# One input tile for all sublayers, U4 ahead of the first transposes, and the memory's products ahead of their stage, in a twelve-sublayer transformer kernel

## The chip, the cores and the metric

The kernel runs on one core of a Trainium2 chip. The metric is the device time of one execution in microseconds (us). A profile is one more execution, taken with the hardware profiler.

## The reference

Three blocks of four sublayers work on one sequence x of 256 rows by 1024 columns, all in float32. Every sublayer normalises x, computes, and adds its result to x:

- block 1: feed-forward f00, convolution module, f01, f10, the gated recurrence hgrn2, f11
- block 2, with shift, scale and gate made from a conditioning vector (adaln): g00, dsa (indexer-selected attention), g01, g10, diff (differential attention), g11
- block 3: pool with attention to a memory of 256 rows, feed-forward m0, moba with attention to the memory, feed-forward m1

What matters here:

```
def swiglu_ffn(x, w_in, w_out):          # f.. and g..: width 2816 or 2752
    gate, up = jnp.split(x @ w_in, 2, axis=-1)
    return (jax.nn.silu(gate) * up) @ w_out

def mem_cross_attention(qm, mem_n, w_mem_kv, q_gain, k_gain):   # in pool and moba
    k, v = jnp.split(mem_n @ w_mem_kv, 2, axis=-1)
    q = rms_norm_3(qm.reshape(B, S, MEM_HEADS, HEAD_DIM), q_gain)
    k = rms_norm_3(k.reshape(B, M, MEM_HEADS, HEAD_DIM), k_gain)
    ...
    p = jax.nn.softmax(s, axis=-1)
    return jnp.einsum('bhsm,bmhd->bshd', p, v)
```

mem_n is the memory normalised with the sublayer's own gain, so the memory's keys and values do not depend on x.

## The kernel before, in words

**Chunks.** All weights are packed into 413 chunks of 1 MB, in the order in which the program takes them (`_plan`, `_ffn_plan`). A U chunk is 1024 rows by 256 columns of an input weight, a W chunk is half of the rows of 512 such columns (two W make two U blocks), and a V chunk is 256 rows by 1024 columns of an output weight. SP's queue loads a chunk into one of three raw buffers (L292). To multiply at close to float32 precision, `_split` makes two parts of each: ACT copies it, rounded, to hi in four pieces of 512 columns (L305), VectorE subtracts, lo = raw - hi, in eight pieces of 256 (L308). There are five buffers of hi and lo each. Every matrix product is three: hi with the input's high part, lo with the high part, hi with the input's low part.

**Products.** The stage's input is the pair `act`, xh and xl: x normalised, transposed to columns and split. A U product (`proj_u`, L517 to L519) has the weight as the stationary operand and gives 128 hidden columns of gate and up for all 256 rows; a chunk has 48 of them. The first four hidden blocks of a stage are made the other way round (`first` and `proj_pair`, L547 to L549): the input is stationary, in two passes, rows 0 to 127 (m = 0) and rows 128 to 255 (m = 1), 48 products each. The second half of the input is needed only in the second pass, and is transposed while the first runs (`split_t(1, ...)`, issued ten products before the pass ends). Their results have rows on partitions, so these four blocks are transposed after Silu and multiplication (L716 to L718), split (L663, L664) and so become the stationary operand hh, hl of the V products (`down`, L588). V products add up in four PSUM banks, and the last four chunks are held back: `finish` runs them for rows 0 to 127, then for rows 128 to 255, and while the second half runs, x of the first is updated, normalised (L413, L418, L419, L460) and, behind the tenth product from the end, transposed (L475) and copied into the next stage's input (L483 and L484, or eight smaller copies L488 and L489 where a shift is added).

**Input tiles.** `new_act` allocates a new pair xh, xl in a pool with one place for each. It is called at the start, for each next stage in `finish`, and in four mixers besides for the output that goes into the output product. A new tile in a place waits until everything that used the old one is done.

**Order in a feed-forward stage.** `ffn` runs `first` (blocks 0 to 3), transposes and splits the hidden blocks 0 to 3, then V0, U4, U5, V1, U6, U7, V2 and so on. In the first and second block's stages it also lets VectorE make adaln's vectors (L1076), piece by piece between chunks.

**The memory.** Its rows are normalised and transposed in the stage before (`mem_norm`, in `first`). `mem_kv` multiplies them (48 products L547 to L549 into ps), copies keys and values out (L1510, L1511), normalises the keys per head (L1462, L394 to L402, L1468, L1474) and transposes them (`to_heads`, L1169, L1174); then it closes the memory's pool, whose place the pool of the stage's own tiles takes over. In `pool` it stands before `first`, in `moba` behind it. moba then makes its keys and queries: copy out (L1191), rotation (L1158 to L1162), norms, transposes, then the next pair's products, chunk pair 2 first.

**Order of the work.** A scheduler orders each engine's instructions ahead of time, from program order and an estimate of when each is ready. An engine then takes its list strictly in order. `issue_after` and `issue(products, n, then)` hold what `then` issues behind the n-th product. `high_priority(300)` lifts the memory's query in `pool` ahead of some other work.

Of the kernel before, what the change touches and what calls it, by code (L numbers as in the profile page):

```python
# [64 lines left out]
def _plan(stages):  # L65
    p = []
    for s in stages:
# [200 lines left out]
class _K:  # L268
# [27 lines left out]
    def _split(self):  # L296
# [9 lines left out]
        for p in range(self.LP):  # L306
            c = slice(2048 // self.LP * p, 2048 // self.LP * (p + 1))
# [32 lines left out]
    def consts(self, act):  # L340
# [29 lines left out]
        self.pending = self.normed(self.x[:, 1], pre)  # L370
# [137 lines left out]
    def proj_u(self, w, act, nb=2):  # L508

        wh, wl = w  # L510
        xh, xl = act
        p = self.ps()
        for b in range(nb):
            o = p[:, 256 * b:256 * b + 256]
            for k in range(8):
                c = slice(256 * k + 128 * b, 256 * k + 128 * b + 128)
                self.nc.tensor.matmul(o, lhsT=wh[:, c], rhs=xh[:, k, :], start=(k == 0), stop=False)  # L517
                self.nc.tensor.matmul(o, lhsT=wh[:, c], rhs=xl[:, k, :], start=False, stop=False)  # L518
                self.nc.tensor.matmul(o, lhsT=wl[:, c], rhs=xh[:, k, :], start=False, stop=(k == 7))  # L519
        return p  # L520
# [106 lines left out]
    def first(self, s, pairs, act):  # L627
# [4 lines left out]
        for m in range(2):  # L632
# [6 lines left out]
            if m == 0:  # L639
# [28 lines left out]
    def ffn(self, s, act):  # L668
        nc, tc = self.nc, self.tc
        nf = 22  # L670
        with tc.tile_pool(name="hp_" + s, bufs=2) as hp:
# [37 lines left out]
            for g in range(2):  # L709
                p = self.ps("tr")  # L710
                for b in range(2):
                    sg = hp.tile([128, 2, 128], F32, name="sg")
                    h = hp.tile([128, 2, 128], F32, name="h")
                    for m in range(2):
                        pp = p4[2 * g + b][m]
                        nc.scalar.activation(sg[:, m], pp[:, :128], AF.Silu)  # L716
                        nc.vector.tensor_tensor(h[:, m], sg[:, m], pp[:, 128:], op=OP.mult)
                        nc.tensor.transpose(p[:, 256 * b + 128 * m:256 * b + 128 * m + 128], h[:, m], self.ident)  # L718
                groups[g] = self.split(p, hp)
            acc = self.new_acc()  # L720
            self.rows_ahead(s)
            for g in range(1, 11):
                for f in (2 * g, 2 * g + 1) if g > 1 else ():
                    w = self.take(("U", s, f))
                    more()
                    hidden(f, self.proj_u(w, act, 1 if s[0] == "g" and f == nf - 1 else 2))
                if g < 8:
                    w = self.take(("V", s, g - 1))
                    more()
                    for m in range(2):  # L730
                        self.down(m, acc[m], w, hs(g - 1), (128, 128), g == 1, False)
# [769 lines left out]
    def mem_kv(self):  # L1501
# [12 lines left out]
        self.scaled(k, rs)  # L1514
        self.to_heads(k, kT)
        self.mem_inner.close()
        return kT, v
# [68 lines left out]
    def moba(self, act):  # L1586
        nc, tc = self.nc, self.tc
        p4 = self.first("moba", _U_ORDER["moba"][:2], act)
        self.rows_ahead("moba")
        kTm, vm = self.mem_kv()  # L1590
        with tc.tile_pool(name="mb", bufs=2) as mp:
# [10 lines left out]
            def key(pp):  # L1602
# [4 lines left out]
                t = mp.tile([128, 2, S], F32, name="kT")  # L1607
                self.to_heads(x, t)
                return t

            def query(pp):
# [3 lines left out]
                t = mp.tile([128, 2, S], F32, name="qT")  # L1615
                self.to_heads(x, t)
                return t, qs
# [105 lines left out]
```

## Time and profile before

| | us |
|---|---|
| median of 3 runs | 2679.16 |
| lowest, highest | 2674.89, 2680.54 |
| the profiled execution | 2686.03 |
| its span, from first to last instruction | 2684.3 |
| VectorE's lo subtractions (L308), 3304 of them | 1188.1 |
| ACT's hi copies (L305), 1652 of them | 945.8 |
| U products (L517 to L519), 8352 of them | 789.7 + 789.0 + 788.3 |
| V products of feed-forward blocks (L588), 2880 of them | 314.6 + 312.9 + 311.1 |

In the profile PE is TensorE, PEld its weight loads, DVE is VectorE, POOL is GpSimd, SP issues the DMAs. A line of a timeline gives start and duration in us, engine, source line, operation, output<-inputs with their shapes, how many instructions are merged into the line, and in brackets how long the engine had been idle before and what it waited for. Neighbouring products overlap in the profile, so their pace is read from their starts. A line of the waits gives engine, operation and line, what was waited for, the total in us, how often, and the longest. A line of the stretches gives the stretch, its length, the busy time and count of PE, PEld, DVE, ACT and POOL, then the granted TensorE clock as a share of full speed, the DMA engines' busy share and GB/s. The averages hide that stages have different limits: what a change is worth is read at the place.

### The profile page before, as it was taken

How to read it: one execution, taken by the hardware profiler on the slowest of the kernel's cores; microseconds unless marked ns; L12 is line 12 of the kernel's file. 1: busy time of each engine (PE TensorE's matmuls, PEld its weight loads, DVE VectorE, ACT ScalarE, POOL GpSimd, SP SyncE). 2: the span in 40 equal slices, each digit the busy share in tenths (PEclk: the TensorE clock that was granted, in tenths of full speed). 3: DMA queues.
4: the chain of work that ended last, by engine and by line, in shares of the span. 5: the costliest groups of instructions: out<-in, count | busy, mean ns of one | idle time of the engine just before them, and what ended most of it. 6: DMA issues, size and time to landing. Idle time of an engine off the chain costs nothing.

```text
span 2684.3 us, 43506 instructions
## 1 busy us (share of the span) xinstructions
PE 2628.1 (98%) x15984; PEld 2307.8 (86%) x15984; DVE 1960.1 (73%) x5536; ACT 1377.8 (51%) x3054; POOL 103.7 (4%) x200
## 2 busy tenths in 40 slices
PE   8999999999999999999999999999999999999999
PEld 7998789989988899899779989977799789877898
DVE  7858887587588885886879678677855866577764
ACT  5445354454554544644665454455644554455543
POOL 0004200000000000000000000000000000000000
PEclk9999899999999999999999999999999999999999
DMA  8744166476434675784448668653554455442452
GB/s 327 291 157 143 65 253 254 173 275 252 156 145 158 252 282 189 266 307 173 173 159 316 240 233 325 219 191 126 206 187 173 169 182 194 173 167 95 175 186 94
DMA packets 91159, 543.62 MB, mean 203 GB/s; under 512 B 10541, under 2 KB 11581, under 8 KB 38082
## 3 DMA queue, kind: packets, MB, share of 16 engines
q1 hardware_dynamic: 90946, 540.85, 55.4%
q8 instruction: 125, 2.05, 0.3%
q14 instruction: 88, 0.72, 0.1%
HBM read 539.69 MB, written 1.13 MB: 201 GB/s over the span
## 4 chain that ended last, share of the span: by engine, by line
issue 46%; PE 42%; DVE 7%; ACT 2%; DMA 2%; POOL 1%; SPq 0%; POOLq 0%; DVEq 0%; ACTq 0%
PE a L588 16%; PE ps L517 7%; PE ps L519 7%; PE ps L518 7%; DVE lo L308 3%; DVE y L828 2%; PE a L548 1%; PE a L549 1%; PE a L547 1%; DMA raw<-in_wall 1%; POOL ry L419 1%; ACT hi L305 1%; ACT junk L413 1%; DMA xn<-modd 1%; DVE xn L460 1%
## 5 line engine op out<-in xcount | busy, mean ns | idle before, releaser
L308 DVE TENSOR_TENSOR lo<-raw,hi 128x256 fp32r<-128x256 f32 x3304 | 1188.1, 419 | 402.4 <-ACT hi L305 402.0
L305 ACT ACTIVATE hi<-raw 128x512 fp32r<-128x512 f32 x1652 | 945.8, 623 | 810.1 <-PE ps L518 269.1
L517 PE MATMUL ps<-xh,hi 128*128 128x256 f32 x2784 | 789.7, 284 | 0.0
L518 PE MATMUL ps<-xl,hi 128*128 128x256 f32 x2784 | 789.0, 283 | 0.0
L519 PE MATMUL ps<-xh,lo 128*128 128x256 f32 x2784 | 788.3, 283 | 0.0
L518 PEld LDWEIGHTS ps<-xl,hi 128*128 128x128 f32 x2784 | 533.3, 192 | 3.8
L517 PEld LDWEIGHTS ps<-xh,hi 128*128 128x128 f32 x2784 | 533.5, 192 | 3.4
L519 PEld LDWEIGHTS ps<-xh,lo 128*128 128x128 f32 x2784 | 533.7, 192 | 0.5
L588 PE MATMUL a<-hi,hh 128*128 128x512 f32 x960 | 314.6, 398 | 2.4 <-ACT hh L663 2.4
L588 PE MATMUL a<-lo,hh 128*128 128x512 f32 x960 | 312.9, 397 | 0.0
L588 PE MATMUL a<-hi,hl 128*128 128x512 f32 x960 | 311.1, 396 | 0.0
L588 PEld LDWEIGHTS a<-lo,hh 128*128 128x128 f32 x960 | 180.3, 188 | 43.5 <-issue 0.2
L588 PEld LDWEIGHTS a<-hi,hl 128*128 128x128 f32 x960 | 180.2, 188 | 43.4
L547 PE MATMUL a<-hi,xh 128*128 128x512 f32 x512 | 203.4, 397 | 8.1 <-ACT xh L483 5.7
L588 PEld LDWEIGHTS a<-hi,hh 128*128 128x128 f32 x960 | 175.0, 188 | 39.5 <-ACT hh L663 3.4
L549 PE MATMUL a<-hi,xl 128*128 128x512 f32 x512 | 202.7, 399 | 1.7 <-DVE xl L489 1.0
L1076 DVE SCALAR_TENSOR_TENSOR adaj<-adaw,cond 128x1024 bf16<-128x1024 f32 x144 | 175.8, 1221 | 37.9 <-DMA adaw<-in_ada 36.7
L548 PE MATMUL a<-lo,xh 128*128 128x512 f32 x512 | 201.6, 394 | 0.5 <-DVE lo L308 0.5
L547 PEld LDWEIGHTS a<-hi,xh 128*128 128x128 f32 x512 | 97.2, 190 | 33.4 <-ACT xh L483 7.4
L549 PEld LDWEIGHTS a<-hi,xl 128*128 128x128 f32 x512 | 96.9, 189 | 27.5 <-DVE xl L484 4.2
L548 PEld LDWEIGHTS a<-lo,xh 128*128 128x128 f32 x512 | 97.1, 190 | 21.8 <-DVE lo L308 1.8
L438 DVE TENSOR_TENSOR upd<-a,pg 128x512 f32<-128x512 f32 x48 | 33.0, 688 | 73.6 <-ACT junk L413 73.6
(352 smaller groups left out, 2743.0 us busy)
## 6 DMA issues: line engine op xcount, KB each, us to landing
raw<-in_wall SPq DMA_DIRECT2D x413, 1024.0 KB, 4.8
adaw<-in_ada SPq DMA_DIRECT2D x144, 512.0 KB, 6.3
G<-in_rows SPq DMA_DIRECT2D x16, 512.0 KB, 4.5
pg<-in_rows SPq DMA_DIRECT2D x12, 512.0 KB, 4.5
xn<-modd SPq DMA_DIRECT2D x12, 512.0 KB, 4.4
cond<-condd SPq DMA_DIRECT2D x7, 512.0 KB, 5.9
memt<-in_mem SPq DMA_DIRECT2D x4, 512.0 KB
x<-in_x SPq DMA_DIRECT2D x2, 512.0 KB, 8.3
```

The source lines that it names most:

```text
L305: self.nc.scalar.activation(h[:, c], r[:, c], AF.Copy)
L308: self.nc.vector.tensor_tensor(l[:, c], r[:, c], h[:, c].bitcast(F32), op=OP.subtract)
L438: nc.vector.tensor_tensor(t, acc[n], pg[:, s], op=OP.mult)
L517: self.nc.tensor.matmul(o, lhsT=wh[:, c], rhs=xh[:, k, :], start=(k == 0), stop=False)
L518: self.nc.tensor.matmul(o, lhsT=wh[:, c], rhs=xl[:, k, :], start=False, stop=False)
L519: self.nc.tensor.matmul(o, lhsT=wl[:, c], rhs=xh[:, k, :], start=False, stop=(k == 7))
L547: yield self.nc.tensor.matmul(p, lhsT=xh[:, k, t], rhs=wh[:, c], start=(k == 0), stop=False)
L548: yield self.nc.tensor.matmul(p, lhsT=xh[:, k, t], rhs=wl[:, c], start=False, stop=False)
L549: yield self.nc.tensor.matmul(p, lhsT=xl[:, k, t], rhs=wh[:, c], start=False, stop=(k == 7))
L588: mm = lambda l, r, i, st, sp: nc.tensor.matmul(acc[i], lhsT=l[:k, t], rhs=r[:k, 1024 * b + 512 * i:1024 * b + 512 * i + 512], start=st, s ...
L828: nc.vector.scalar_tensor_tensor(c, hp[:, j, t:t + S], w(t), c, op0=OP.mult, op1=OP.add)
L1076: self.nc.vector.scalar_tensor_tensor(junk, self.ada_w.pop(n), 1.0, self.cond, op0=OP.mult, op1=OP.mult, accum_out=self.mods[k][:, c:c + 1])
```

## The change

Five edits. (1) `new_act` makes the pair once and returns the same objects ever after. (2) In the feed-forward stages of f and g kind, U4 comes directly behind the first four blocks; their transposes and splits are issued behind U4's 20th product, then V0, U5, V1 and on as before. Silu and multiplication of all four blocks stand ahead of that; their results lie in two places of the hh and hl buffers. (3) In `pool` and `moba` the memory's products and norms come first, then the stage's `first`, then the transposes of the memory's keys; moba multiplies chunk pair 2 before it transposes its first keys and queries. (4) In the six mixers, memory chunks included, lo is made in four pieces of 512 columns. (5) At the start both halves of x are transposed before the first product in program order, and `first` of f00 issues none.

```
@@ _ffn_plan: W(0,1) W(2,3) U4 V0 U5 V1 U6 U7 V2 ...
+        if g == 2:
+            out.insert(-1, ("V", tag, 0))
-        if 0 < g < ng - 3:
+        if 1 < g < ng - 3:
             out.append(("V", tag, g - 1))
@@ _plan
-                at = 4 if s == "moba" else 0
-                us[at:at] = _w("mem0" if s == "pool" else "mem1", 0, 1)
+                us[:0] = _w("mem0" if s == "pool" else "mem1", 0, 1)
@@ _split
-        for p in range(self.LP):
-            c = slice(2048 // self.LP * p, 2048 // self.LP * (p + 1))
+        lp = self.LP if self.plan[i][1][0] in "fg" or self.plan[i][1] in ("m0", "m1") else self.LP // 2
+        for p in range(lp):
+            c = slice(2048 // lp * p, 2048 // lp * (p + 1))
             self.nc.vector.tensor_tensor(l[:, c], r[:, c], h[:, c].bitcast(F32), op=OP.subtract)
@@ consts
-        self.pending = self.normed(self.x[:, 1], pre)
+        self.split_t(1, self.normed(self.x[:, 1], pre), act)
+        self.pending = None
@@ new_act
-        return (self.act.tile([128, 8, 256], F32R, name="xh"), self.act.tile([128, 8, 256], F32R, name="xl"))
+        if self.the_act is None:
+            self.the_act = (self.act.tile([128, 8, 256], F32R, name="xh"), self.act.tile([128, 8, 256], F32R, name="xl"))
+        return self.the_act
@@ proj_u: its loop is now the generator u_products
+        p = self.ps()
+        self.issue(self.u_products(w, act, p, nb))
+        return p
@@ first
-            if m == 0:
+            if m == 0 and self.pending:
@@ ffn
-            for g in range(2):
-                p = self.ps("tr")
-                for b in range(2):
...
-                        nc.tensor.transpose(p[:, 256 * b + 128 * m:256 * b + 128 * m + 128], h[:, m], self.ident)
-                groups[g] = self.split(p, hp)
-            acc = self.new_acc()
+            hts = []
+            for f in range(4):
+                sg = hp.tile([128, 2, 128], F32, name="sg")
+                if f % 2 == 0:
+                    ht = hp.tile([128, 2, 2, 128], F32, name="hh" if f == 0 else "hl", bufs=4)
+                h = ht[:, f % 2]
+                for m in range(2):
+                    pp = p4[f][m]
+                    nc.scalar.activation(sg[:, m], pp[:, :128], AF.Silu)
+                    nc.vector.tensor_tensor(h[:, m], sg[:, m], pp[:, 128:], op=OP.mult)
+                hts.append(h)
+            def turn():
+                for g in range(2):
+                    p = self.ps("tr")
+                    for b in range(2):
+                        for m in range(2):
+                            nc.tensor.transpose(p[:, 256 * b + 128 * m:256 * b + 128 * m + 128], hts[2 * g + b][:, m], self.ident)
+                    groups[g] = self.split(p, hp)
...
+                    products = self.u_products(w, act, p, 1 if s[0] == "g" and f == nf - 1 else 2)
+                    if f == 4:
+                        self.issue(products, 20, turn)
+                    else:
+                        self.issue(products)
+                    hidden(f, p)
+                    if f == 4:
+                        acc = self.new_acc()
+                    if f == 4 or (f % 2 and g < 8):
+                        j = 0 if f == 4 else g - 1
+                        w = self.take(("V", s, j))
...
@@ mem_kv ends ahead of the transposes
+        return k, kT, v
+
+    def mem_keys(self, k, kT):
         self.to_heads(k, kT)
         self.mem_inner.close()
@@ pool
-        kT, v = self.mem_kv()
+        k, kT, v = self.mem_kv()
+        p4 = self.first("pool", _U_ORDER["pool"], act)
+        self.mem_keys(k, kT)
         with tc.tile_pool(name="po", bufs=2) as pp:
-            p4 = self.first("pool", _U_ORDER["pool"], act)
@@ moba
+        km, kTm, vm = self.mem_kv()
         p4 = self.first("moba", _U_ORDER["moba"][:2], act)
+        self.mem_keys(km, kTm)
         self.rows_ahead("moba")
-        kTm, vm = self.mem_kv()
...
-            k, q, mq = key(p4[0]), query(p4[1]), self.mem_query(1, mp, p4[2])
+            kq = [key_x(p4[0]), query_x(p4[1])]
+            pk, pq = chunks(2)
+            k, q = turned(kq[0], "kT"), turned(kq[1], "qT")
+            mq = self.mem_query(1, mp, p4[2])
             v = self.evac(mp, p4[3], "v")
             er = weights(k, q)
-            pk, pq = chunks(2)
```

`key_x` and `query_x` are the old `key` and `query` without their transposes, and `turned` makes these.

More of the change, by code (lines that the diff above doesn't have):

```diff
@@ L504, in new_act, with u_products @@
     def new_act(self):
-        return (self.act.tile([128, 8, 256], F32R, name="xh"), self.act.tile([128, 8, 256], F32R, name="xl"))
+        if self.the_act is None:
+            self.the_act = (self.act.tile([128, 8, 256], F32R, name="xh"), self.act.tile([128, 8, 256], F32R, name="xl"))
+        return self.the_act
     def proj_u(self, w, act, nb=2):
+        p = self.ps()
+        self.issue(self.u_products(w, act, p, nb))
+        return p
+    def u_products(self, w, act, p, nb=2):
         wh, wl = w
         xh, xl = act
-        p = self.ps()
         for b in range(nb):
@@ L516, in proj_u @@
                 c = slice(256 * k + 128 * b, 256 * k + 128 * b + 128)
[L517 to L520, printed above, removed]
+                yield self.nc.tensor.matmul(o, lhsT=wh[:, c], rhs=xh[:, k, :], start=(k == 0), stop=False)
+                yield self.nc.tensor.matmul(o, lhsT=wh[:, c], rhs=xl[:, k, :], start=False, stop=False)
+                yield self.nc.tensor.matmul(o, lhsT=wl[:, c], rhs=xh[:, k, :], start=False, stop=(k == 7))
     def proj_tile(self, w, act, p, m, at):
@@ L708, in ffn @@
             p4 = self.first(s, ((0, 1), (2, 3)), act)
-            for g in range(2):
-                p = self.ps("tr")
-                for b in range(2):
[L712 to L718, printed above, removed]
-                groups[g] = self.split(p, hp)
@@ L721, in ffn @@
+            def turn():
[5 more added lines that the diff above has]
+                    groups[g] = self.split(p, hp)
             self.rows_ahead(s)
-            for g in range(1, 11):
-                for f in (2 * g, 2 * g + 1) if g > 1 else ():
+            acc = None
@@ L724, in ffn @@
+            for g in range(2, 11):
+                for f in (2 * g, 2 * g + 1):
                     w = self.take(("U", s, f))
                     more()
[L726 to L731, printed above, removed]
+                    p = self.ps()
+                    products = self.u_products(w, act, p, 1 if s[0] == "g" and f == nf - 1 else 2)
[9 more added lines that the diff above has]
+                        w = self.take(("V", s, j))
+                        more()
+                        for m in range(2):
+                            self.down(m, acc[m], w, hs(j), (128, 128), j == 0, False)
@@ L1600, in moba, with key_x @@
             chunks = lambda i: self.vprojs("moba", _U_ORDER["moba"][i], act)
-            def key(pp):
+            def key_x(pp):
                 x = self.evac(mp, pp, "q")
@@ L1606, in key, with query_x @@
                 self.scaled(x, rs)
[L1607 to L1611, printed above, removed]
+                return x, None
+            def query_x(pp):
                 x = self.evac(mp, pp, "q")
@@ L1614, in query, with turned @@
                 self.rope(x.rearrange("p m (h d) -> p m h d", h=4), 4, tabs["mq"], 64, mp)
-                t = mp.tile([128, 2, S], F32, name="qT")
-                self.to_heads(x, t)
-                return t, qs
+                return x, qs
+            def turned(xs, name):
+                t = mp.tile([128, 2, S], F32, name=name)
+                self.to_heads(xs[0], t)
+                return t if xs[1] is None else (t, xs[1])
+            key = lambda pp: turned(key_x(pp), "kT")
+            query = lambda pp: turned(query_x(pp), "qT")
             def weights(kT, q):
@@ L1676, in run @@
         self.mem_due = False
+        self.the_act = None
         act = self.new_act()
```

1 line of the change is left out of this document (removed).

## The prediction

> **What bounds the kernel now.** I read the page first, then TensorE's list of waits, then the busy time and granted clock of a few stretches, and last the timeline around each wait that the diff can reach.
>
> ```profile
> span 2684.3 us, 43506 instructions
> PE 2628.1 (98%) x15984; PEld 2307.8 (86%) x15984; DVE 1960.1 (73%) x5536; ACT 1377.8 (51%) x3054; POOL 103.7 (4%) x200
> ```
>
> The profiled execution took 2686.03 us, 1.7 us more than its span and 0.26% more than the median of the runs shown, 2679.16. TensorE is busy for 98% of the span, and the diff removes no product. So the span can shrink only by the 56 us in which TensorE stands idle and by the stretches in which it runs slowly. Its waits say what stands behind the idle time (columns: total us, times, longest):
>
> ```profile
> PE a L547 <- ACT xh L483: 5.7, 4, 1.8
> PE tr L1169 <- issue: 5.4, 1, 5.4
> PE tr L718 <- DVE h L717: 3.8, 4, 1.3
> ...
> PE a L588 <- ACT hh L663: 2.4, 2, 1.3
> ...
> PE tr L1169 <- DVE memkk L1474: 2.4, 1, 2.4
> ...
> PE a L549 <- DVE xl L489: 1.0, 1, 1.0
> ```
>
> These six rows, 20.7 us, are the places that the diff moves. After three of them the clock drops (the column before the DMA share is the granted clock; busy us of PE, PEld, DVE, ACT and POOL stand ahead of it):
>
> ```profile
> 573.90:577.30 3.40, 3.40 (x10) 2.55 (x10) 2.21 (x8) 1.92 (x4) 0.00 (x0) 0.50 0.93 384
> 2106.50:2109.90 3.40, 3.24 (x10) 2.79 (x11) 0.44 (x2) 1.26 (x3) 0.13 (x1) 0.50 0.85 325
> 2406.90:2420.50 13.60, 11.90 (x42) 7.57 (x43) 12.37 (x70) 9.01 (x29) 0.00 (x0) 0.50 0.01 2
> 2126.00:2144.00 18.00, 16.96 (x108) 13.48 (x107) 17.84 (x65) 11.53 (x30) 0.25 (x2) 1.00 0.30 114
> ```
>
> The first stretch lies behind the start of f10, the second behind the memory's keys in pool, the third follows the wait in moba. The last is the middle of pool, where VectorE is busy for 17.84 of 18 us: there it, not TensorE, sets the pace.
>
> **Part 1, the first feed-forward blocks (eight stages).** Before, the first V products follow directly on the first product pass, and need transposes, Silu and split of the four hidden blocks. In f10:
>
> ```profile
> 568.92 0.39 PE L549 MATMUL a<-hi,xl 128*128 128x512 f32 x1
> ...
> 569.94 0.28 PE L517 MATMUL ps<-xh,hi 128*128 128x256 f32 x1
> 570.06 0.28 PE L518 MATMUL ps<-xl,hi 128*128 128x256 f32 x1
> 571.64 0.33 PE L718 MATMUL tr<-ident,h 128*128 128x128 f32 x1 [1.30 <-DVE h L717]
> 572.22 0.63 ACT L305 ACTIVATE hi<-raw 128x512 fp32r<-128x512 f32 x1 [2.59 <-DMA raw<-in_wall]
> 573.38 0.50 PE L588 MATMUL a<-hi,hh 128*128 128x512 f32 x1 [1.19 <-ACT hh L663]
> 573.97 0.47 DVE L717 TENSOR_TENSOR h<-sg,a 128x128 f32<-128x128 f32 x2
> ```
>
> The last product of the pass starts at 568.92; U products come 0.12 us apart. The change puts U4 there, and the transposes behind its 20th product, 20 x 0.12 = 2.4 us later. What must end within that is Silu and multiplication of the last half-blocks: two ACT and two DVE instructions, about 1 us if nothing stands ahead of them. The other 28 products of U4 (3.4 us) cover the split. So the rows L718 and L588 of the waits, 3.8 + 2.4 = 6.2 us, go; with f10's stop its half-clock stretch goes, worth at most half of 3.4 us, taken as 1.5. What comes late next are the transposes themselves where an adaln multiplication or a piece of a split stands ahead on VectorE; I leave 0.15 us a stage, 1.2 in all. Nothing is added: the same 33 weight chunks, the same eight transposes, and the weight loads keep their places in SP's queue but for V0, now one chunk later. Sum: -6.2 - 1.5 + 1.2 = -6.5. Bounds: -7.7, and +27 by the third rival.
>
> **Part 2, one input tile.** Where a mixer's output was in the old tile, the new one could be written only when the last product had read the old one. At the end of pool:
>
> ```profile
> 2166.08 1.04 PE L475 MATMUL tr<-ident,xn 128*128 128x128 f32 x8
> ...
> 2169.03 0.40 PE L588 MATMUL a<-hi,xl 128*128 128x512 f32 x1
> ...
> 2170.37 1.06 ACT L483 ACTIVATE xh<-tr 128x512 fp32r<-128x512 f32 x2
> 2171.00 0.50 PE L547 MATMUL a<-hi,xh 128*128 128x512 f32 x1 [1.56 <-ACT xh L483]
> ```
>
> The transposes stood complete at 2167.1, and ACT copied them out only at 2170.37, behind the last product of 2169.03. With one object the copy of rows 0 to 127 clashes only with products that read those rows, which all ran in the half before; it can start some 3 us earlier, and the wait of 1.56 us goes. Of the row's 5.7 us the longest wait, 1.8, is the program's start and stays; 3.9 go in conv, pool and moba, and the 1.0 of L489 in dsa. Left over: 0.4. Sum -4.5, bounds -4.9 and -2. In hgrn the output has tiles of its own. A gain beyond these waits is excluded, since TensorE stands still nowhere else there for that reason.
>
> **Part 3, pool.** The memory's key transposes move from before the first product pass to behind it.
>
> ```profile
> 2107.81 0.33 SPq L1542 DMA_DIRECT2D invc<-in_k_invc  x1
> 2107.86 0.13 POOL L1554 MEMSET u<- 128x32 f32 x1 [14.92 <-PE tr L1169]
> 2120.71 0.42 DVE L1468 TENSOR_TENSOR q<-a,small 128x256 f32<-128x256 f32 x1
> 2125.64 0.16 DVE L402 SCALAR_TENSOR_TENSOR rs<-rs_w,rs 128x8 f32<-128x8 f32 x1
> ```
>
> The wait of 2.4 us for memkk goes (the keys' chain then has the 96 products of the pass to end in), and its half-clock stretch (at most half of 3.4 us; taken 1.4, as four of its ten are transposes). But the two upper rows show what hangs on those transposes: the first writes of stage tiles, a DMA and a POOL memset, come right behind them. The stage's tiles take over the memory pool's place. Moved behind the pass, they hold back SP (invc and wg), POOL's memset and the whole query of the memory, whose last steps ran from 2120.71 to 2125.80 beside products of the pass. Behind the two DMAs on SP stand the next weight loads, and for those ACT's hi copies; invc was issued 0.05 us ahead of the memset, as soon as the hold ended, so I cost that at nothing, and at most at the 2.59 us that a late load cost in part 1. That query's VectorE work (a reduction, two products of 0.42, thirteen steps of 0.16: about 3.5 us) now falls into the stretch where VectorE is the bound; some of it fits into the places of lo pieces that can run earlier, so I take 2.3. Sum: -2.4 - 1.4 + 2.3 = -1.5. Bounds -3.8 (all of it hidden) and +4: the chain's whole length, 6 us with the reduction ahead of it, and one more half-clock stretch, 1.7.
>
> **Part 4, moba.** The same hold, the other way round:
>
> ```profile
> 2398.24 0.66 PE L1169 MATMUL tr<-ident,memkk 128*128 128x128 f32 x4
> 2399.43 0.66 ACT L1191 ACTIVATE q<-a 128x256 f32<-128x256 f32 x2
> 2402.42 0.39 PE L548 MATMUL ps<-lo,xh 128*128 128x512 f32 x1
> 2402.64 0.39 PE L549 MATMUL ps<-hi,xl 128*128 128x512 f32 x1
> 2408.48 0.45 PE L1169 MATMUL tr<-ident,q 128*128 128x128 f32 x1 [5.44 <-issue]
> ```
>
> The stage's own keys are copied out of PSUM only at 2399.43, right behind memkk again, though TensorE is by then far into chunk pair 2 and had done the memory's products between. From memkk to the key's transpose pass 2408.48 - 2398.24 = 10.2 us; behind memkk's transposes TensorE had 4.1 us of products left, 18 at 0.23, the last at 2402.64, and then stood for 5.4. After the change the memory's products and their chain lie ahead of the stage's pass, memkk is transposed right behind that pass, and all 48 products of pair 2 (10.9 us) stand ahead of the key's transpose. 10.9 covers 10.2: the stop goes, and with it the cause of 13.6 us at clock 0.50. How much the clock returns is bounded by VectorE, busy for 12.37 of those 13.6 us: if VectorE sets the pace from memkk on, the gain is what memkk moves ahead, the 30 products of pair 2 that ran before it, 30 x 0.23 = 6.9; if TensorE does, it is 5.4 plus up to 4. Between 6.9 and 9.4, nearest the lower since VectorE is nearly full: -7.5, bounds -9.4 and -4.
>
> f10's two stops of 1.30 and 1.19 us and pool's 2.4 were each followed by 3.4 us at 0.50, as moba's 5.4 was by 13.6. The Trainium skill's page TensorE: Matmul & The Clock Gate (section Why this matters for your kernels) asks for no idle gaps over about 3 us, since an idle window halves the clock; the trace is stricter in f10 and pool. By the page alone their 1.5 and 1.4 would not come back, and the sum would be -18.1.
>
> **Part 5, lo pieces.** 85 of the 413 weight chunks lie in the six mixers.
>
> ```profile
> 2111.74 1.29 DVE L484 TENSOR_TENSOR xl<-tr,xh 128x512 fp32r<-128x512 f32 x2 [2.98 <-ACT xh L483]
> 2117.43 2.77 DVE L308 TENSOR_TENSOR lo<-raw,hi 128x256 fp32r<-128x256 f32 x8 [4.40 <-ACT hi L305]
> ```
>
> Eight 256-wide pieces take 2.77 us; two 512-wide subtractions 1.29, so four about 2.5. That is 0.27 us a chunk, 23 us of VectorE in all, nearly all hidden behind TensorE. Against it, an instruction queued behind a piece waits up to 0.27 us longer. Taken -1; bounds -5, if a fifth of it reaches TensorE, and +3, if a dozen such waits lie on its path.
>
> **Part 6, the start.** Both halves of x are transposed before the first product in program order. The second half's eight transposes leave the pass (0.8 us by the 1.04 that eight take in part 2's first row, less the last one's tail), but its two copies, 2 x 0.53 on ACT by the same fence, and its subtractions (1.29, part 5) now stand among the first splits, for which TensorE waits there. I take 0, bounds -1 and +2.4, those three rows' sum.
>
> **Sum.** -6.5 - 4.5 - 1.5 - 7.5 - 1 + 0 = -21.0. On the profiled execution 2686.0 - 21.0 = 2665.0; on the median 2679.2 - 21.0 = 2658.2 us.
>
> **Rivals.** First, *VectorE keeps the mixers*: pool comes out at its bound, +4, moba returns only 4, part 5 nothing. -6.5 - 4.5 + 4 - 4 = -11, 2668 us. For it: 17.84 of 18 us. Against: VectorE idled 2.98 us before 2111.74, inside the pass, where its work can move. Chance 0.18. Second, *more comes back*: moba -9.4, pool -3.8, part 5 -5, the rest as forecast: -29, 2650 us. For it: VectorE is full in pool and moba, so its relief counts there; against: each part would have to reach its end. Chance 0.11. Third, the slow side, *the new transposes wait at U4's 20th product*: TensorE takes its queue in order, so U4's other 28 products stand behind the transposes. In f10 the last two h ended at 574.44, because ACT had stood on a late weight load (2.59 us); the new transposes would be due at about 571.55. If their place in the queues stays so, each of eight stages stops for 2.9 us (23 us), each stop costs a half-clock stretch (1.5 each, 12), and 7.7 are saved: +27, with the other parts +13, 2692 us. It decides against the change from about 2.8 us a stage with the clock staying up. Against it: in the new program order all four h stand ahead of every split of hidden blocks, before they stood behind the first. Chance 0.05. Fourth, *the change does not do what it says*: writes still wait for the whole tile (part 2 gives 0), and the transposes land in the queue where they were (part 1 gives 3); pool +1, moba -4: -6, 2673 us. Against it: already before, rows 128 to 255 were written inside the pass whose products read rows 0 to 127 of the same tile. Chance 0.07.
>
> **How the numbers follow.** The forecast gets the remaining 0.59. From no change a measurement here can tell about 0.2%, 5.4 us, close to the 5.7 between the highest and the lowest of the three runs. Forecast and the first two rivals are faster by more (0.88, less 0.04 for a first rival that comes out worse); the fourth is split, 0.02 to faster, 0.05 to same; the third is slower. Faster 0.86, same 0.09, slower 0.05. The range takes in the unknown parts' bounds and reaches from 2646, the second rival less the 4 us by which its other parts may still be off, to 2674, just past the fourth.
>
> **What would show it.** Right: L718 and L588 waits under 1.5 us together; L547 waits for xh near 2 us, the start's; no TensorE stop of over 1 us at moba's key, no clock of 0.50 there or in f10; 340 512-wide lo pieces; memory-query steps of pool behind the last product of the pass. Wrong: waits of L718 on h of over 2 us in several stages, a stop behind pool's pass of over 4 us, or new half-clock stretches.

## The result, and the profile after

| | median, us (runs) | profiled execution, us | its span | granted clock |
|---|---|---|---|---|
| before | 2683.37 (19) | 2686.03 | 2684.3 | 0.991 |
| changed | 2671.46 (19) | 2675.0 | 2672.9 | 0.989 |

The ratio of changed to before is 0.9949, with a 95% interval of 0.9931 to 0.9967: on 2683.4 us that is 13.7 us less, between 8.9 and 18.5. The prediction had 2658.2 in a range of 2646 to 2674, so the direction and the range held; its -21 us, a ratio of 0.9922, lies outside the interval. The page of the changed kernel begins so:

```profile
span 2672.9 us, 43146 instructions
...
PE 2630.4 (98%) x15984; PEld 2312.8 (87%) x15984; DVE 1938.7 (73%) x5196; ACT 1378.1 (52%) x3054; POOL 105.3 (4%) x200
```

TensorE does the same 15984 instructions and is busy for 2.3 us longer than before; VectorE has 340 instructions and 21.4 us less to do, and the time follows neither. In TensorE's waits (L718 is now L736, L588 is L598, L547 is L557, L483 is L487, L1169 is L1197), three rows matter:

```profile
PE tr L736 <- DVE hl L728: 4.1, 4, 2.8
...
PE a L557 <- ACT xh L487: 1.8, 1, 1.8
...
PE tr L1197 <- DVE q L1496: 1.1, 1, 1.1
```

Gone are the waits of the first V products for hh and of pool's transposes for memkk. Of the kernel before's four waits for copies of the input tile (L483, now L487) only the program's start is left, as forecast. But the new transposes wait 4.1 us, 2.8 of it at once, and there is a new wait behind pool's pass. The stretches that answer to the prediction's (f10's first blocks; the middle of pool; moba from its key on):

```profile
563.00:568.00 5.00, 5.00 (x35) 4.57 (x34) 5.00 (x17) 4.72 (x11) 0.00 (x0) 1.00 0.80 310
2116.70:2133.77 17.07, 16.75 (x42) 10.60 (x43) 12.35 (x56) 8.00 (x19) 0.25 (x2) 0.50 0.22 87
2399.00:2412.60 13.60, 12.73 (x53) 8.09 (x52) 12.02 (x59) 11.08 (x33) 0.00 (x0) 0.75 0.22 79
```

f10 runs through at full clock. Moba has no long stop and half of its half-clock time is left. Pool, however, now has 17 us at clock 0.50, which the kernel before did not have; TensorE is busy for 16.75 of them and VectorE for 12.35.

To find the place of gains and losses I take the length of a stage, from the start of its first product to that of the next stage. For all executions that are told of below (m0 and moba stand together, since the memory's products moved from one to the other):

| | f01 | hgrn | dsa | diff | pool | m0+moba |
|---|---|---|---|---|---|---|
| before | 190.5 | 155.8 | 110.8 | 127.7 | 73.7 | 326.0 |
| changed | 192.7 | 158.3 | 113.1 | 129.5 | 76.8 | 318.2 |
| changed, a second profile | 189.9 | 157.6 | 109.8 | 129.8 | 69.9 | 318.3 |
| 256-wide lo pieces | 192.3 | 155.5 | 110.6 | 126.3 | 70.1 | 320.9 |
| two input tiles | 190.1 | 158.3 | 110.6 | 128.9 | 78.7 | 317.8 |
| old first blocks | 191.3 | 157.6 | 109.6 | 132.6 | 69.9 | 318.1 |
| old pool | 192.4 | 159.9 | 109.8 | 130.1 | 69.1 | 315.2 |
| old moba | 194.0 | 158.8 | 109.4 | 132.1 | 77.0 | 330.0 |
| old start | 189.9 | 158.0 | 109.3 | 129.8 | 69.9 | 315.4 |
| keys inside pool's pass | 192.4 | 157.8 | 109.9 | 129.9 | 68.2 | 315.9 |
| the same, 256-wide in hgrn, diff | 189.9 | 155.7 | 112.2 | 125.3 | 68.3 | 315.4 |
| the same, turn at 40 in f01 | 191.1 | 155.6 | 109.7 | 122.7 | 68.4 | 315.5 |
| before, with the new moba | 196.1 | 155.9 | 110.7 | 123.5 | 72.1 | 322.2 |

Read down a column: pool takes either 70 or 77 us with the same code, and f01 either 190 or 192 to 194. Others move without an edit too. With one order of instructions in moba, m0 and moba take 315.2 to 315.9 us in five profiles, and 318.1 to 318.3 in the three that have 6.83 us at clock 0.50 there. Dsa takes 109.3 to 109.9, or 112.2 and 113.1 with such stretches, and diff, with one order, differs by 4 to 5 us. So a difference of less than about 4 us between two lines of the table is an effect of the edit only where rows show it or many profiles agree.

### The profile page after: what moved, and what is told of

Its sections match the earlier page's. It is cut to its first block, busy times and chain, and to the rows that moved or that the text cites. A ratio compares the mean times of both kernels' runs of the same rounds, so it can differ in the third digit from the quotient of the medians.

```text
span 2672.9 us, 43146 instructions
## 1 busy us (share of the span) xinstructions
PE 2630.4 (98%) x15984; PEld 2312.8 (87%) x15984; DVE 1938.7 (73%) x5196; ACT 1378.1 (52%) x3054; POOL 105.3 (4%) x200
## 4 chain that ended last, share of the span: by engine, by line
PE 56%; issue 35%; DVE 5%; ACT 2%; POOL 1%; DMA 1%; SPq 0%; POOLq 0%; ACTq 0%
PE a L598 20%; PE ps L528 8%; PE ps L530 8%; PE ps L529 8%; PE a L557 2%; PE a L559 2%; PE a L558 2%; DVE y L856 2%; DVE lo L311 1%; PE a L1237 1%; PE tr L479 1%; POOL ry L423 1%; PE ps L558 1%; PE ps L557 1%; PE ps L559 1%
## 5 line engine op out<-in xcount | busy, mean ns | idle before, releaser
L311 DVE TENSOR_TENSOR lo<-raw,hi 128x256 fp32r<-128x256 f32 (+1 forms) x2964 | 1160.3, 450 | 409.2 <-ACT hi L306 408.8
L598 PE MATMUL a<-hi,hh 128*128 128x512 f32 x960 | 309.6, 396 | 0.0
L598 PE MATMUL a<-hi,hl 128*128 128x512 f32 x960 | 309.2, 396 | 0.0
L598 PE MATMUL a<-lo,hh 128*128 128x512 f32 x960 | 309.2, 396 | 0.0
L598 PEld LDWEIGHTS a<-lo,hh 128*128 128x128 f32 x960 | 179.9, 188 | 43.7
L598 PEld LDWEIGHTS a<-hi,hl 128*128 128x128 f32 x960 | 179.9, 187 | 43.5
L557 PE MATMUL a<-hi,xh 128*128 128x512 f32 x512 | 202.0, 396 | 3.4 <-ACT xh L487 1.8
L598 PEld LDWEIGHTS a<-hi,hh 128*128 128x128 f32 x960 | 173.9, 188 | 35.6 <-ACT hh L673 0.2
L557 PEld LDWEIGHTS a<-hi,xh 128*128 128x128 f32 x512 | 97.0, 189 | 26.4 <-ACT xh L492 5.2
```

The costliest lines, as they stand in the source:

```text
L311: self.nc.vector.tensor_tensor(l[:, c], r[:, c], h[:, c].bitcast(F32), op=OP.subtract)
L557: yield self.nc.tensor.matmul(p, lhsT=xh[:, k, t], rhs=wh[:, c], start=(k == 0), stop=False)
L598: mm = lambda l, r, i, st, sp: nc.tensor.matmul(acc[i], lhsT=l[:k, t], rhs=r[:k, 1024 * b + 512 * i:1024 * b + 512 * i + 512], start=st, s ...
```

## The experiments

Each ratio is to the kernel before, run beside the experiment. In the three sets of runs its medians were 2685.77, 2690.30 and 2683.22 us, so kernels of different sets are compared by ratio.

**The changed kernel once more.** No edit.

> The changed kernel itself, profiled a second time. Theory 'clock by grid': the half-clock stretches all begin and end on a grid of 3.41 us that lies differently in each execution, and a stretch follows where one slot of the grid holds little TensorE work, so that the same stop lowers the clock in one execution and not in another; then stages without long stops repeat within 0.3 us, and pool, dsa and diff can change by 2 to 7 us, pool to 70 if its stop of 1.24 us is split between two slots. Rival 'set by the program': the same stages show the same stretches, pool 76.8 with 17 us at 0.50, dsa 113.

It took 2662.75 us, pool 69.9 instead of 76.8, dsa 109.8 instead of 113.1. All stretches at 0.50, in every profile here, are one or several times 3.41 us long, and lie on a grid of that step, which stands elsewhere in each execution. Busy time and clock by slots of that grid, behind the end of pool's pass, first for the changed kernel's first profile, then for its second:

```profile
2113.29:2116.70 3.41, 1.89 (x11) 1.01 (x9) 3.19 (x11) 3.15 (x8) 0.12 (x1) 1.00 0.99 372
2116.70:2120.11 3.41, 3.20 (x9) 2.04 (x10) 2.67 (x14) 2.31 (x6) 0.00 (x0) 0.50 0.98 389
```

```profile
2107.64:2111.05 3.41, 2.08 (x12) 1.14 (x10) 3.19 (x11) 2.96 (x8) 0.12 (x1) 1.00 0.97 371
2111.05:2114.46 3.41, 2.65 (x13) 1.62 (x14) 3.41 (x19) 3.09 (x9) 0.00 (x0) 1.00 1.00 401
```

The second column of numbers is TensorE's busy time. With 1.89 us of 3.41 in a slot, the next slot is at half speed; with 2.08 it isn't. Five more profiles have this order of TensorE's work in pool. The old moba's and the old start's:

```profile
2116.22:2119.63 3.41, 1.68 (x10) 0.85 (x8) 3.18 (x14) 3.41 (x9) 0.12 (x1) 1.00 0.95 365
2119.63:2123.04 3.41, 3.25 (x10) 1.92 (x9) 2.79 (x16) 2.19 (x7) 0.00 (x0) 0.50 0.93 372
```

```profile
2108.00:2111.42 3.42, 2.07 (x12) 1.40 (x11) 3.12 (x7) 2.81 (x8) 0.12 (x1) 1.00 0.98 381
2111.42:2114.83 3.41, 2.96 (x15) 1.64 (x14) 3.41 (x18) 3.37 (x9) 0.00 (x0) 1.00 1.01 396
```

With two input tiles the slot held 1.68 and the clock fell; with the old first blocks it held 2.06, with 256-wide pieces 2.12, and the clock stayed. So three of seven executions lose about 7 us in pool. What the program sets is a stop of 1.1 to 1.3 us behind memkk's transposes, and shorter ones of 0.2 to 0.4 us behind it; whether they fall into one slot of the grid is chance. The rival, that the program sets the stretch, is out.

Outside pool the busy time of a slot does not tell what follows. In the changed kernel's first profile f01's stop leaves 1.61 us in a slot, and the clock stays; a slot of moba holds 2.54, and it falls:

```profile
375.90:379.31 3.41, 1.61 (x14) 1.61 (x15) 1.95 (x7) 3.30 (x7) 0.00 (x0) 1.00 0.96 404
379.31:382.72 3.41, 3.41 (x25) 3.14 (x24) 3.38 (x9) 1.45 (x5) 0.00 (x0) 1.00 0.26 55
2400.01:2403.42 3.41, 2.54 (x17) 1.81 (x16) 2.98 (x17) 3.14 (x9) 0.00 (x0) 1.00 0.74 267
2403.42:2406.83 3.41, 3.41 (x10) 1.68 (x8) 2.26 (x15) 3.41 (x12) 0.00 (x0) 0.50 0.10 41
```

Five profiles with the same order of moba have such a slot, with 2.54 to 2.61 us, and keep the clock behind it.

**Old pool: part 3 undone.**

```diff
+        self.mem_keys(k, kT)
         p4 = self.first("pool", _U_ORDER["pool"], act)
-        self.mem_keys(k, kT)
```

> Only part 3 is undone: the memory's key transposes stand ahead of pool's pass again. Theory 'the hold costs more than the wait': pool's length falls from 76.8 us to 73.7, the value of the kernel before, or below it; the wait of 2.4 us for memkk is back with at most 3.4 us of half clock behind it, and the 17 us at clock 0.50 behind the pass are gone; kernel about 2668. Rival, the forecast's part 3 (-1.5 for the new place): pool's length was set by something else in the change (512-wide pieces, order of splits), so it rises to 78, kernel 2673.

Median 2666.68 us, ratio to before 0.9924 (0.9902 to 0.9946); pool 69.1. The wait for memkk is back, but shorter than the 2.4 us of the kernel before, and no clock is lost:

```profile
2097.21 0.63 PE L1197 MATMUL tr<-ident,memkk 128*128 128x128 f32 x4 [0.88 <-DVE memkk L1502]
```

The theory holds in its direction: against the changed kernel's 69.9 without a stretch, the old place is 0.8 us better, in one profile. That it cannot lose clock is not shown: in the kernel before, its stop of 2.4 us was followed by 3.4 us at 0.50.

**Keys inside pool's pass.** The transposes are issued behind the eighth product of the pass's second half, so the stage's tiles come free there.

```diff
+        keys = 8, lambda: self.mem_keys(k, kT)
+        p4 = self.first("pool", _U_ORDER["pool"], act, keys)
-        p4 = self.first("pool", _U_ORDER["pool"], act)
-        self.mem_keys(k, kT)
... in first, for the second half
+                self.issue(chain.from_iterable(steps), *(then if m else ()))
-                self.issue(chain.from_iterable(steps))
```

> The changed kernel with one move: in pool the memory's key transposes are issued behind the eighth product of the pass's second half, some 9 us earlier than in the changed kernel, so that the stage's tiles come free inside the pass. Theory 'the hold costs': the query's steps run beside the second half, no stop and no half clock behind the pass, and pool takes 71 to 73 us, less than in both kernels; kernel about 2667. Rival 'VectorE sets pool's pace': the same VectorE work is only earlier, the middle of pool stays near 30 us behind the pass, and pool stays at 75 to 77; kernel about 2671. If the keys are late there, TensorE stops inside the pass, and pool gets longer.

Median 2666.84, ratio 0.9921 (0.9893 to 0.9948); pool 68.2, less than expected. The middle of pool in this kernel:

```profile
2105.00:2135.00 30.00, 28.69 (x171) 23.25 (x170) 29.45 (x98) 19.82 (x46) 0.25 (x2) 1.00 0.38 133
```

VectorE is busy for 29.45 of 30 us, and so is TensorE for 28.69: the fuller VectorE of the rival is real, but did not keep the stage long. From 76.8 to 68.2, 1.7 us are the hold on the stage's tiles (69.9 to 68.2), the rest the clock.

**256-wide lo pieces: part 5 undone.**

```diff
-        lp = self.LP if self.plan[i][1][0] in "fg" or ... else self.LP // 2
+        lp = self.LP
```

> Only part 5 is undone: the mixers' lo pieces are 256 wide again. In the changed kernel's trace hgrn, dsa and diff are longer than before by 2.6, 2.3 and 1.8 us, and no other part of the change names them. Theory 'long pieces delay': with 256-wide pieces the three come back by at least 1.5 us each (hgrn 156 to 157, dsa 111, diff 128) and the kernel gets about 5 us faster, near 2666. Rival 'pieces are harmless', the forecast's -1: the three stay within 0.8 us of 158.3, 113.1 and 129.5, VectorE gets some 23 us busier, and the kernel takes 0 to 2 us more, about 2672. Second rival 'clock': the stages move by several us with half-clock stretches that come and go at places without any long wait.

Median 2667.36, ratio 0.9946 (0.9918 to 0.9975), no different from the changed kernel's. By stages, against the second profile of the changed kernel: hgrn 2.1 and diff 3.6 us shorter, m0 and moba 2.6 longer, conv and dsa 0.8 longer each. So both theories are half right, and the sum is near nothing. Some of diff's 3.6 us is the second rival's, the clock: 6.83 us of diff are at 0.50 here, 10.24 there. But all profiles agree that both stages are shorter with 256-wide pieces: hgrn takes 155.5 to 155.9 us in five, 157.6 to 159.9 with long pieces in eight, and diff 122.7 to 127.7 against 128.9 to 132.6. In hgrn, the changed kernel's VectorE and TensorE:

```profile
852.50 2.49 DVE L311 TENSOR_TENSOR lo<-raw,hi 128x512 fp32r<-128x512 f32 x4
854.91 1.29 DVE L1038 TENSOR_TENSOR sg<-sg,small 128x512 f32<-128x512 f32 x2
856.11 1.29 DVE L1040 TENSOR_TENSOR on<-on,sg 128x512 f32<-128x512 f32 x2
```

```profile
856.85 1.26 PE L502 MATMUL tr<-ident,on 128*128 128x128 f32 x8 [1.12 <-DVE on L1040]
```

Four long pieces, 2.49 us, stand ahead of on, and the transposes of on wait 1.12 us. With 256-wide pieces six of them, 2.09 us, stand there, and TensorE does not wait (no idle time is noted in this row):

```profile
857.37 0.66 PE L502 MATMUL tr<-ident,on 128*128 128x128 f32 x4
```

In moba it is the other way round. With 256-wide pieces a softmax is written ahead of the copy of the attention's output on ACT, and TensorE stops for about 4 us; the kernel before with the new moba, below, shows the rows. The width of a piece changes not only times but the order in which the program is written, and in moba it is this order that costs the 4 us.

**Two input tiles: part 2 undone.** new_act again allocates both tiles at each call.

> Only part 2 is undone: each sublayer allocates its input tile anew. Forecast, -4.5 for the one object: TensorE's first products wait again for ACT's copy at conv to f01, pool to m0 and moba to m1 (1 to 2 us each) and for VectorE's at dsa to g01 (1.0); conv, pool, moba and dsa lengthen by 1 to 2 us each, 4 to 5 in all; the median goes up by as much, to about 2676. Rival 'the copies wait anyway': the waits and stage lengths stay as in the changed kernel within 0.5 us, because writes still wait for the whole tile there, and the gain of the changed kernel came from elsewhere.

Median 2674.22, ratio 0.9937 (0.9912 to 0.9963). The waits are back at all four places, TensorE's first product in f01, the third in g01, and the first in m0 and m1:

```profile
350.39 0.50 PE L554 MATMUL a<-hi,xh 128*128 128x512 f32 x1 [0.46 <-ACT xh L487]
...
1383.31 0.50 PE L556 MATMUL a<-hi,xl 128*128 128x512 f32 x1 [1.01 <-DVE xl L493]
...
2167.33 0.50 PE L554 MATMUL a<-hi,xh 128*128 128x512 f32 x1 [1.60 <-ACT xh L487]
...
2485.10 0.50 PE L554 MATMUL a<-hi,xh 128*128 128x512 f32 x1 [2.21 <-ACT xh L487]
```

0.46 + 1.01 + 1.60 + 2.21 = 5.3 us, against 4.5 forecast. The ratio cannot be told from the changed kernel's 0.9949; the rows show the waits.

**Old first blocks: part 1 undone**, the function ffn and its plan as before.

> Only part 1 is undone: the first V products follow directly on the first product pass again. Forecast, -6.5 for the new order: TensorE's waits at the transposes of h and at the first V products come back (3.8 and 2.4 us in sum over eight stages), f10 gets 3 to 4 us longer with its half-clock stretch, f00, g00 and g10 about 0.8 each; f01 gets 2 us shorter, as its stop of 2.9 us at the new transposes goes; sum of the eight stages +5 to +7, median about 2677. Rival, a grown third rival: the stop in f01 and the later split cost as much as the new order saves, sum within 1.5 us of the changed kernel, median within 2 us.

Median 2673.93, ratio 0.9948 (0.9921 to 0.9975), again not to be told from the changed kernel's. Two rows of its waits:

```profile
PE tr L726 <- DVE h L725: 4.6, 5, 1.5
...
PE a L596 <- ACT hh L671: 0.6, 1, 0.6
```

The eight stages together take 1536.0 us, against 1531.0 in the changed kernel's second profile and 1534.2 in its first: 5.0 us more, or 1.9 where f01 had its stop. In the other eight profiles with the new order they take 1531.3 to 1535.7 us. f10 took 191.2 here, no longer than with the new order: its stops of 1.30 and 1.19 us in the kernel before came behind a late weight load, for which ACT waited 2.59 us, and here the load is not late. A late load decides f01 too. ACT in f01, in the changed kernel's first profile, and TensorE's row, then ACT in the second profile:

```profile
372.23 0.26 ACT L727 ACTIVATE sg<-a 128x128 f32<-128x128 f32 x1
376.01 1.15 ACT L306 ACTIVATE hi<-raw 128x512 fp32r<-128x512 f32 x2 [3.52 <-DMA raw<-in_wall]
377.07 0.26 ACT L727 ACTIVATE sg<-a 128x128 f32<-128x128 f32 x1
```

```profile
377.70 0.33 PE L736 MATMUL tr<-ident,hl 128*128 128x128 f32 x1 [2.75 <-DVE hl L728]
```

```profile
373.64 1.15 ACT L306 ACTIVATE hi<-raw 128x512 fp32r<-128x512 f32 x2 [0.72 <-DMA raw<-in_wall]
374.70 0.26 ACT L727 ACTIVATE sg<-a 128x128 f32<-128x128 f32 x1
```

A hi copy stands ahead of the last Silu. In the first profile it waits 3.52 us for its load and TensorE stops for 2.75; in the second 0.72, and f01 takes 189.9. That is the third rival's mechanism, in one stage and in five of the ten profiles with the new order (there ACT waits 3.1 to 3.5 us, and f01 takes 192.3 to 194.0). The old order has the same weakness: in the kernel before with the new moba, below, ACT waits 2.83 us there, the first V products 2.8, and f01 takes 196.1.

**Old moba: part 4 undone.** The memory's products, key transposes and keys as before; the rest is the changed kernel.

> Only part 4 is undone: moba's pass first, then the memory's products, key transposes and keys as before. Forecast, -7.5 for the new order: m0 and moba together come out 7 to 9 us longer than 318.2, TensorE stops again for over 4 us at the transpose of moba's key with 13 us at clock 0.50 behind it; kernel about 2679. Rival 'VectorE keeps moba': 4 us longer, because the other parts (512-wide pieces, one input tile) already gave the rest; kernel about 2675.

Median 2681.21, ratio 0.9990 (0.9968 to 1.0012): without part 4 the gain is gone. m0 and moba take 330.0 us, 11.8 more (with 13.65 us at clock 0.50, against 6.83 in the changed kernel), and longer than in the kernel before, because a second stop is there beside the one that was expected:

```profile
PE tr L1198 <- DVE rs_w L405: 5.5, 1, 5.5
PE a L599 <- ACT xh L1209: 4.1, 2, 3.8
```

**Before, with the new moba: part 4 alone.**

> The kernel before with part 4 alone: the memory's products ahead of moba's pass, its key transposes behind it, pair 2 ahead of the keys. Forecast, -7.5 for this part: m0 and moba together 318 to 319 us (326.0 before), no stop at the transpose of moba's key, median 7 to 8 us below before. Theory 'the parts support each other': undoing it in the changed kernel cost 11.8 us, 4 of it by a stop of 4.0 us at the output products; if that stop belongs to the old order, m0 plus moba falls to 314 to 316. Rival 'VectorE keeps moba': 256-wide pieces leave no room for more, and it falls by 4 only, to 322.

Median 2682.97, ratio 0.9998 (0.9975 to 1.0022): by itself the part gives nothing that can be measured. m0 and moba fall from 326.0 to 322.2, and the stop at moba's key is gone, but the second stop is here too. The end of its ACT queue (between the rows left out stand more exponentials), and TensorE's row:

```profile
2451.82 0.49 ACT L1226 ACTIVATE e<-e,mx,rs 128x128 f32<-128x128 f32 x1 [2.26 <-DVE mx L1222]
...
2456.08 1.06 ACT L1179 ACTIVATE xh<-tr 128x512 fp32r<-128x512 f32 x2
```

```profile
2456.71 0.72 PE L587 MATMUL a<-hi,xh 128*128 128x512 f32 x2 [3.84 <-ACT xh L1179]
```

Eight exponentials, 4.3 us, stand ahead of the copy that the output's products need. In the changed kernel the copies stand ahead of them. The number expected by "VectorE keeps moba" came out, but not its reason: what the rows show is this stop, an order on ACT. That the stop belongs to the old order alone is refuted too. It comes with the new moba and 256-wide pieces, and with the old moba and 512-wide ones; with neither edit, in the kernel before, and with both, in the changed kernel, it is absent. So undoing one of the two costs more than it alone had brought.

**Old start: part 6 undone.** The second half of x is transposed inside f00's first pass again.

> Only part 6 is undone: the second half of x is transposed inside f00's first pass again. Forecast, 0 for the new start (bounds -1 and +2.4): f00's length and the time of its first product stay within 1 us of the changed kernel's 192.4 to 193.3 and 11.2 to 11.3. Rival 'the early copies delay the first splits': the first product starts 1 to 2 us earlier and f00 stays as long, so that the kernel gains that much.

It took 2660.8 us. The first product starts at 11.22 us (11.32 and 11.15 in the changed kernel), and f00 takes 194.3, against 193.3 and 192.4, and 192.0 to 193.5 in all ten profiles with the new start. So the new start gains 1 to 2 us of f00; the rival is out.

**256-wide pieces in hgrn and diff only, keys inside pool's pass.**

```diff
+        lp = self.LP // 2 if self.plan[i][1] in ("conv", "dsa", "pool", "moba", "mem0", "mem1") else self.LP
```

> The changed kernel with pool's key transposes behind the eighth product of the pass's second half, and with 256-wide lo pieces in hgrn and diff alone; conv, dsa, pool, moba and the memory keep 512. Theory 'long pieces delay': hgrn near 155.5 and diff near 126.5 (158 and 130 with long pieces), the wait of 1.3 to 1.5 us for on in hgrn and g11's wait of 2.7 us for xn down to 1.5 go with it; pool 68 and m0 plus moba 316 as with the earlier keys; kernel about 2660, some 6 us under the kernel with the earlier keys alone. Rival 'pieces are harmless, the stages moved by the clock': hgrn and diff stay at 158 and 130 in the absence of a stretch, kernel about 2667.

Median 2658.08, ratio 0.9874 (0.9833 to 0.9916), less than the changed kernel's whole interval. hgrn 155.7 and diff 125.3 as expected, pool 68.3, m0 and moba 315.4. TensorE's wait for on falls from 1.3 us to 0.5. Some of diff's gain is again the clock: 3.41 us of it are at 0.50, over 10 in the kernel with the earlier keys alone. The intervals of these two kernels overlap.

**The same with f01's transposes behind U4's 40th product.**

```diff
-                        self.issue(products, 20, turn)
+                        self.issue(products, 40 if s == "f01" else 20, turn)
```

> The kernel with earlier keys and 256-wide pieces in hgrn and diff, and in f01 alone the eight transposes of the hidden blocks behind U4's 40th product instead of its 20th. Theory 'third rival in one stage': f01's stop of 2.5 to 2.9 us, when ACT stands on a late weight load, shrinks to below 0.8 us, since 20 more products, 2.4 us, lie ahead of it; f01 is 190 in every execution, and the median about 1 us under the kernel without this move, near 2657. Rival 'the split comes late instead': the last eight products, 1 us, don't cover the split of the hidden blocks, TensorE waits about 1.5 us at the first V product, and f01 takes 191.5 or more.

Median 2655.88, ratio 0.9894 (0.9865 to 0.9922), the same as without it within the intervals. In this execution the load came on time, so the theory's case did not arise. What the rival names did, with 1.02 us for the 1.5 expected:

```profile
380.64 0.73 PE L598 MATMUL a<-hi,hl 128*128 128x512 f32 x2 [1.02 <-DVE hl L674]
```

f01 takes 191.1, 1.1 more than with the load on time and 20 products. Whether it pays when the load is late stays open. This kernel's profile has the shortest span, with the fewest half-clock slots:

```profile
span 2647.1 us, 43296 instructions
```

## Why the prediction was right, and where it was wrong

The direction was right, and for most of the stated reasons; the size was too large. Part by part, from single profiles and mostly against the changed kernel's second one: -5.0 (first blocks), -5.3 (one input tile, by its waits), +0.8 (pool), -11.8 (moba), +1.4 (lo pieces, the sum of the differences above, with pool and rounding), -1.9 (start), together -21.8. That this is close to the forecast of -21 is luck. The second profile's execution lies 8.7 us below its kernel's median, the profile of before 2.7 above its own: of the 23.3 us between the two executions 11.9 are left, the distance of the medians.

Most of the spread goes with the granted clock. In the 19 runs of the changed kernel the time falls from 2681.84 us at a clock of 0.988 to 2657.68 at 0.996. An estimate from all recorded runs that state a clock, with one slope for all kernels, is 2.4 us for each 0.001. At a clock of 0.992 it gives, to within 1 to 2 us:

| kernel | us at clock 0.992 |
|---|---|
| before, in three sets | 2682.2 to 2683.1 |
| changed | 2670.7 |
| old first blocks | 2674.6 |
| two input tiles | 2673.4 |
| old pool | 2671.4 |
| old moba | 2679.7 |
| 256-wide lo pieces | 2669.7 |
| before, with the new moba | 2682.3 |

So at equal clock the change gains about 12 us, a little less than the 13.7 measured: it was not lost clock that kept it from 21. Undone one by one, the parts are worth 3.9 (first blocks), 2.7 (input tile), 0.7 (pool), 9.0 (moba) and -1.0 us (lo pieces); of these only the first two and moba are clear of the error. What a part changes in the clock itself is left out of these numbers. The forecast had put the first blocks and the input tile too high, and expected gains from pool and from the lo pieces that are not there. Why the waits of parts 1 and 2 weigh less in the whole kernel than in their own stages stays open.

- **Part 1**, -6.5: -5.0 by its stages, -3.9 at equal clock. The old waits go as forecast. What failed is the 1.5 for f10's clock: I took one execution's late load for a property of the program. The 1.2 us for the new transposes in all eight stages are 2.0 with the load on time and 4.1 with it late, 2.75 of it in f01; my first sign of being right, under 1.5, failed both times.
- **Part 2**, -4.5: -5.3 by its waits, just beyond its bound of -4.9, since m1's wait is 2.21 and not 1.8; -2.7 at equal clock. The mechanism is as written.
- **Part 3**, -1.5: +0.8 without a stretch, +7.7 with one, against one profile of the old place; the ratios of the two places, 0.9949 and 0.9924, have intervals that overlap. This is the step whose mechanism failed. I counted the steps that the hold moves behind the pass as VectorE time (2.3 us, at most 4 with one half-clock stretch of 1.7), and expected VectorE to set the pace there. In its place TensorE ran out of work: 1.08 us behind memkk's transposes, for the query that the hold delays, and where that fell into one slot, the clock was down for five slots in a row. TensorE, busy for 16.75 of 17.07 us, then set the pace itself.
- **Part 4**, -7.5: -11.8 in the changed kernel's stages, beyond its bound of -9.4, and -9.0 at equal clock; alone -3.8 in its stages and nothing in the median. The stop at the key went, as forecast. What was missing is the order on ACT at the stage's end, which the edits changed and the trace of before does not show.
- **Part 5**, -1: near +1.4, inside its bounds, though not from the cause I gave: two stages lose 2 to 4 us to pieces, order and clock, three gain.
- **Part 6**, 0: a gain of 1 to 2 us in f00, beyond the bound of -1.
- **The rivals.** The first, -11 us, comes nearest to the 13.7 measured, but its moba number, 4 us, is that of the part alone, and its reason, VectorE, is not what the rows show, by pool's 12.35 of 17.07 us and by the kernel with the earlier keys, where VectorE was full and the stage short. Of the second, moba gave more than forecast, pool and the lo pieces did not. The third came true in f01 alone. The fourth is out by the returned waits of part 2.
- **The clock.** The last of my signs of error, new half-clock stretches, came true in pool. The Trainium skill's page TensorE: Matmul & The Clock Gate (section Why this matters for your kernels) asks for no idle gaps of over about 3 us. Here no single gap of pool is longer than 1.3 us, and the clock fell in three of seven executions: the measurement is the stricter. What goes with it in pool is the work within a slot of 3.41 us, 1.89 us and less against 2.06 and more; f01 and moba, above, show that this is no general rule.

## What to carry to other kernels

Before a stall's price is taken from one profile, ask whether its cause, a late load or a drop of the clock, is the program's or that execution's; profile the same kernel twice, and compare stage by stage. Where every run comes with its granted clock, compare times at equal clock: the spread of runs shrinks, and effects of 3 to 4 us show that the medians hide. Where small steps close a memory pool, put them where TensorE still has products queued, not at the end of a pass: the tiles behind the pool decide when the next stage may begin. An edit that changes the size of small steps may act through the order in which the program is then written, so undo it stage by stage and keep it only where it helps.

## What the runs showed of the hardware

- The granted clock changes on a grid of 3.41 us, with a phase of its own in each execution. In pool, a slot with 1.68 to 1.89 us of TensorE work was followed by half clock, three times of three; one with 2.06 to 2.12 was not, four times of four. Elsewhere a slot with 1.61 kept the clock (f01), and one with 2.54 lost it (moba). A stop of the same length costs 0 or 7 us by where it falls.
- A weight load for which ACT waits came 2.8 us later in one execution than in another of the same kernel (3.52 against 0.72 us of ACT's idle time). The loads around it were issued at about the same times (362.0 and 371.9 us, 362.5 and 372.3) and took 6.7 and 7.9 us to land in place of 5.0 and 5.2; why, these runs don't show.
